# Expert biases as one float32r product of high and low parts, and the residual kept only as its two parts

## The chip, the cores and the metric

The kernel runs on one core of a Trainium2 chip. The metric is device time in microseconds (us), the median of the runs shown; less is better. TensorE (PE) multiplies, VectorE (DVE), ScalarE (ACT) and GpSimd (POOL) work on whole tiles, SyncE (SP) issues most of the DMAs. Each engine takes its instructions in order. "PEld" in the profile is TensorE's loading of weights, which runs beside its products.

## What is computed

One layer of a decoder on 256 tokens of 1024 columns, in float32: token mixing (sparse attention, a sliding window, a gated merge, an output projection, a residual), then 32 experts of which each token uses four, a second residual and a last norm. The change lies in the second half:

```python
def clamped_swiglu(gu):
    x_glu, x_lin = gu[..., ::2], gu[..., 1::2]
    x_glu = jnp.minimum(x_glu, SWIGLU_LIMIT)
    x_lin = jnp.clip(x_lin, -SWIGLU_LIMIT, SWIGLU_LIMIT)
    return x_glu * jax.nn.sigmoid(SWIGLU_ALPHA * x_glu) * (x_lin + 1.0)
...
    def body(y, blk):
        tok, g, e = blk
        xb = ht[tok]
        hid = clamped_swiglu(xb @ w_up[e] + b_up[e])
        out = hid @ w_down[e] + b_down[e]
        return y.at[tok].add(out * g[:, None]), None
...
    x = x + ga1 * (merged @ w_out[l])
    h = rms_norm(x, g_ffn[l]) * (1.0 + sc2) + sh2
    x = x + ga2 * moe_ffn(h, w_router[l], b_router[l], w_up[l], b_up[l], w_down[l], b_down[l])
    return rms_norm(x, g_final)
```

## The kernel before

Attention takes about the first 245 us. Then the router picks the experts, and the 32 experts follow, each with up to 64 tokens. Their weights, 12 chunks of 1 MB per expert (8 up, 4 down), come through 18 slots in SBUF, issued by SyncE as slots come free. The steps of one expert, with the lines of the kernel before:

- Every four experts, `gather` makes one-hot rows of their tokens (`oh`, L838), multiplies them with `xh` and `xl` (L850; the norms at L826), and VectorE and ScalarE turn the result into `XT` (L852, L853). `xh` and `xl` are the high and low parts of the residual x, made in the first part from `xt` (ScalarE's cast at L762, the differences on GpSimd at L764 and L768).
- `up`: for each of the two halves `n` of the hidden units, the bias opens the sum in PSUM (L891: a column of the identity, broadcast, picks one row of `rows` on 64 partitions; gate and linear columns go to two halves of the array, so two products for each n), then four chunks follow (L904), four float32 products each.
- `act`: swiglu for each half (L801, L803, L805 to L807, on VectorE and ScalarE), two transposes (L914) and a copy into `hTe` (L915).
- `down`: four chunks (L924), the first two into the bank "z", the last two into "o". Each bank's sum is cast to float32r by ScalarE (`ohi`, L930), and VectorE makes the difference (`olo`, L931).
- `combine`: scatter products of the high and the low part (L938, L939), four pairs, and VectorE adds each, times the gate, to `y` (L941).

A float32 product counts as two records in the trace, a float32r product as one: a chunk's four up products are x8 there, a down chunk is x16, a bias x8 per expert.

Before expert 16 all engines meet at a branch (L962): a loop over tokens beyond the 64 of an expert, which is not entered here. Its condition is read from `count`.

At the end the second residual comes in: `y` times `g2b` (L1075) plus `xt` (L1076), for both halves of the tokens, then the last expert's down products (L1085) a quarter of the columns at a time, with the last norm behind them, written over `xt` (L1106, L1113, L1115) and out.

The order of the instructions on each engine is not that of the text: a scheduler with a timeline of its own puts them in order when the kernel is built, and an engine then keeps that order, waiting where an operand is late. `issue_after` and one dependency by hand (L891's second half for expert 0, the chunks of expert 16) are the only hints.

Of the kernel before, what the change touches and what calls it, by code (L numbers as in the profile page):

```python
# [10 lines left out]
F32 = mybir.dt.float32  # L11
F32R = mybir.dt.float32r
# [9 lines left out]
SL = 64  # L22
# [58 lines left out]
def _layout(inp):  # L81
# [6 lines left out]
    def pairs(a, b):  # L88
        """blocks of 128 columns by row: [block, column, a | b, row]"""
        return np.stack([a, b], axis=2).reshape(8, 128, 2048)  # L90

    def twos(a):
        """two blocks of 128 columns by row"""
        return a.reshape(4, 2, 128, D).transpose(0, 2, 1, 3).reshape(4, 128, 2048)
# [63 lines left out]
def tile_trunk(ctx: ExitStack, tc: tile.TileContext, A, out: bass.AP, dbg=None):  # L158
# [65 lines left out]
    def residual(i, q, slots):  # L224
        """two blocks of 128 columns of the modulation of a residual"""
# [6 lines left out]
    def across(g, out, tag="pt"):  # L232
        """a vector of columns, on all partitions"""
# [12 lines left out]
    # =====================================================================  # L246
    # token mixing
    # =====================================================================
    with tc.tile_pool(name="front", bufs=1) as fr:
# [5 lines left out]
        def split(src, n, pool=0):  # L255
            """float32 as an exact sum of two float32r parts; the last columns' difference on GpSimd"""
# [14 lines left out]
        # conditioning  # L271
# [8 lines left out]
        # the conditioning vector on all partitions  # L280
# [3 lines left out]
        # rms norm and transposes of x  # L284
# [7 lines left out]
        # relative bias of 16 heads by distance  # L292
# [26 lines left out]
        def modulation(i, k, scale, shift, g):  # L319
            """a block of 128 columns of a scale (times g) and a shift"""  # L320
# [8 lines left out]
        # projections, those with the columns on partitions: kc vc | ksl kw | qn0..3 | qs0..3, and with the tokens  # L329
        # there: vsl vw vs. Each float32 product is three of float32r parts, the product of the low parts being  # L330
        # below float32's last place
# [36 lines left out]
        # as Hankel tiles: the query rows run backwards  # L368
# [20 lines left out]
        def backwards(ap):  # L389
            """the queries of each half in reverse"""  # L390
            return bass.AP(tensor=ap.tensor, offset=ap.offset + 127, ap=[list(z) for z in ap.ap[:-1]] + [[-1, 128]])
# [18 lines left out]
        # branch gates (their eight partial sums in four groups of partitions)  # L410
# [17 lines left out]
        # kc, vc: halves of the partitions take the even and the odd tokens' rows  # L428
# [24 lines left out]
        def transposed(tiles, cols, eng):  # L453
            """the blocks' transposes, side by side: [keys, block, queries]"""
# [14 lines left out]
        def weights(a):  # L469
            """softmax of the selected and window branches, with the branches' gates"""  # L470
# [38 lines left out]
        def compressed(a, po):  # L509
            """closes the sum of the three branches"""  # L510
# [3 lines left out]
            # compressed branch  # L514
# [26 lines left out]
        def sliding(a):  # L541
# [3 lines left out]
            # sliding window with sinks  # L545
# [31 lines left out]
        # ks  # L577
# [9 lines left out]
        # compressed keys and values, hidden layer  # L587
# [19 lines left out]
        # compressed keys and values, second layer  # L607
# [30 lines left out]
        # merge gates, second modulation  # L638
# [21 lines left out]
        # branches' projections, merge  # L660
# [27 lines left out]
        # output projection, residual, router with the second modulation in its weights  # L688
# [81 lines left out]
        # the logits' eight partial sums are in four groups of partitions  # L770
# [27 lines left out]
    def swiglu(pool, gu):  # L798
        """of half of the hidden units"""
# [10 lines left out]
    # =====================================================================  # L810
    # experts
    # =====================================================================
    g2b = fixed([128, D], F32, "g2b", "qn")
    with tc.tile_pool(name="moe", bufs=1) as mo:
# [6 lines left out]
        def norms(oh):  # L821
            """the norms of the slots' tokens, on all partitions"""
# [312 lines left out]
```

## Time and profile before

| | us |
|---|---|
| median of 3 runs | 1216.19 |
| lowest, highest | 1215.51, 1217.31 |
| span of the profiled execution | 1211.7 |
| TensorE busy in it | 1148.3 |
| VectorE, ScalarE, GpSimd busy | 491.8, 234.6, 135.5 |
| weights' DMA (queue of SyncE), share of 16 engines | 93.1% |

The profiled execution's own time is its span; what lies around it is the difference to the median, 4.5 us. Busy time of TensorE includes the modelled ends of pipelined products, so 95% does not say that it never waits: its timeline, start against start, does. Rows of the timeline give the start, the duration, the engine, the line, the operation, the tiles (out<-in), the shapes, the number of instructions merged into the row, and in brackets the idle time before and who ended it.

### The profile page before, as it was taken

How to read it: one execution, taken by the hardware profiler on the slowest of the kernel's cores; microseconds unless marked ns; L12 is line 12 of the kernel's file. 1: busy time of each engine (PE TensorE's matmuls, PEld its weight loads, DVE VectorE, ACT ScalarE, POOL GpSimd, SP SyncE). 2: the span in 40 equal slices, each digit the busy share in tenths (PEclk: the TensorE clock that was granted, in tenths of full speed). 3: DMA queues.
4: the chain of work that ended last, by engine and by line, in shares of the span. 5: the costliest groups of instructions: out<-in, count | busy, mean ns of one | idle time of the engine just before them, and what ended most of it. 6: DMA issues, size and time to landing. Idle time of an engine off the chain costs nothing. (4 is left out here: it accounts for less than half of the span.)

```text
span 1211.7 us, 16366 instructions
## 1 busy us (share of the span) xinstructions
PE 1148.3 (95%) x6645; PEld 587.2 (48%) x6646; DVE 491.8 (41%) x1041; ACT 234.6 (19%) x535; POOL 135.5 (11%) x115
## 2 busy tenths in 40 slices
PE   6999998989999999999999987999999999999996
PEld 5867768934345434434444433445444444443443
DVE  7958687641343332322322232233222323233334
ACT  3346453321102011201111101101111110111002
POOL 4726474400000000000000000000000000000001
PEclk8999998989999999999999998999999999999999
DMA  9988555879999999999999999999999999999993
GB/s 384 412 310 325 209 209 176 314 306 403 388 421 416 422 421 421 421 420 421 421 421 421 421 416 371 420 422 420 422 420 421 422 420 422 421 421 421 420 422 148
DMA packets 66608, 463.79 MB, mean 383 GB/s; under 512 B 7216, under 2 KB 9408, under 8 KB 11744
## 3 DMA queue, kind: packets, MB, share of 16 engines
q1 hardware_dynamic: 66016, 461.84, 93.1%
q8 instruction: 54, 0.88, 0.3%
q10 hardware_dynamic: 512, 0.85, 0.2%
q14 instruction: 26, 0.21, 0.0%
HBM read 461.59 MB, written 1.07 MB: 382 GB/s over the span
## 5 line engine op out<-in xcount | busy, mean ns | idle before, releaser
L904 PE MATMUL z<-chunk,XT 128*64 128x512 f32 x2048 | 476.5, 599 | 0.0
L904 PEld LDWEIGHTS z<-chunk,XT 128*64 128x64 f32 x2048 | 143.9, 137 | 261.9 <-issue 243.0
L941 DVE SCALAR_TENSOR_TENSOR y<-s,gates,y 128x512 f32<-128x512 f32 x124 | 90.9, 748 | 118.9 <-PE s L939 116.3
L924 PE MATMUL z<-chunk,hTe 128*64 128x256 f32 x992 | 124.2, 383 | 8.3 <-ACT hTe L915 8.3
L924 PE MATMUL o<-chunk,hTe 128*64 128x256 f32 x992 | 122.8, 382 | 0.0
L801 DVE TENSOR_SCALAR g<-z 128x256 f32<-128x256 f32 x64 | 27.1, 424 | 234.9 <-PE z L904 234.9
L1106 POOL TENSOR_TENSOR xt<-y,gfb 128x512 f32<-128x512 f32 x3 | 3.9, 1293 | 954.9 <-ACT sq L1105 952.4
L265 POOL TENSOR_TENSOR hilo<-chunk,hilo 128x576 fp32r<-128x576 f32 (+4 forms) x49 | 93.1, 1916 | 78.3 <-ACT hilo L261 55.6
L924 PEld LDWEIGHTS z<-chunk,hTe 128*64 128x64 f32 x992 | 70.6, 136 | 57.9 <-issue 14.6
L803 ACT ACTIVATE th<-g 128x256 f32<-128x256 f32 x64 | 26.7, 416 | 356.8 <-DVE g L801 356.8
L924 PEld LDWEIGHTS o<-chunk,hTe 128*64 128x64 f32 x992 | 71.4, 137 | 39.0 <-issue 6.3
L891 PE MATMUL z<-rows,kc 64*64 64x512 f32 x256 | 67.2, 624 | 6.4 <-PEq L962 6.4
L931 DVE TENSOR_TENSOR olo<-z,ohi 128x512 fp32r<-128x512 f32 x31 | 21.4, 691 | 118.6 <-ACT ohi L930 118.6
L340 PE MATMUL z<-hh,hilo 128*128 128x256 f32 x184 | 53.0, 295 | 8.5 <-ACT hh L350 8.5
L938 PE MATMUL s<-ohi,oht 128*128 128x512 f32 x124 | 56.1, 468 | 4.1 <-DVE y L941 2.7
L261 ACT CAST hilo<-chunk 128x1024 fp32r<-128x1024 f32 (+1 forms) x49 | 49.4, 1029 | 29.9 <-PE z L676 10.0
L341 PE MATMUL z<-hh,hilo 128*128 128x256 f32 x184 | 52.9, 291 | 0.0
L324 DVE SCALAR_TENSOR_TENSOR chunk<-chunk,condrow 128x1024 f32<-128x1024 f32 x32 | 51.3, 1638 | 1.0 <-DMA chunk<-in_wada 1.0
L915 ACT COPY hTe<-pt 128x256 f32<-128x256 f32 x64 | 23.6, 371 | 144.6 <-PE pt L914 144.5
L342 PE MATMUL z<-hl,hilo 128*128 128x256 f32 x184 | 50.8, 290 | 0.8 <-DVE hl L351 0.7
L938 PEld LDWEIGHTS s<-ohi,oht 128*128 128x128 f32 x124 | 22.2, 187 | 57.9 <-issue 35.7
L939 PE MATMUL s<-olo,oht 128*128 128x512 f32 x124 | 48.7, 408 | 0.0
(302 smaller groups left out, 1282.2 us busy)
## 6 DMA issues: line engine op xcount, KB each, us to landing
chunk<-in_wup SPq DMA_DIRECT2D x256, 1024.0 KB, 19.8
chunk<-in_wdn SPq DMA_DIRECT2D x127, 1024.0 KB, 19.8
chunk<-in_wada SPq DMA_DIRECT2D x24, 1024.0 KB, 12.3
chunk<-in_wing SPq DMA_DIRECT2D x8, 1024.0 KB, 6.8
chunk<-in_win SPq DMA_DIRECT2D x7, 960.0 KB, 17.0
chunk<-in_w SPq DMA_DIRECT2D x4, 1024.0 KB, 12.0
chunk<-in_wbr SPq DMA_DIRECT2D x4, 1024.0 KB, 5.3
chunk<-in_wout SPq DMA_DIRECT2D x4, 1024.0 KB, 5.6
```

Of the source, the lines that this page charges most:

```text
L261: ACT.copy(hi[:, 0:n], src)
L265: POOL.tensor_tensor(lo[:, d:n], src[:, d:n], hi[:, d:n].bitcast(F32), op=OP.subtract)
L324: V.scalar_tensor_tensor(w[:, b], w[:, b], 1.0, condrow, op0=OP.mult, op1=OP.mult, accum_out=m[:, b:b + 1])
L340: PE.matmul(o, wh, hh[:, k], start=start, stop=False)
L341: PE.matmul(o, wl, hh[:, k], start=False, stop=False)
L342: PE.matmul(o, wh, hl[:, k], start=False, stop=stop)
L891: PE.matmul(gu[n][64 * c:64 * c + 64], ident[0:64, 2 * e + c:2 * e + c + 1].to_broadcast([64, 64]), rows[0:64, n * 512:(n + 1) * 512], sta ...
L904: PE.matmul(gu[n][64 * c:64 * c + 64], XT[:, 2 * j + k, c0:c0 + 64], w[:, k, c], start=False, stop=j == 3 and k == 1)
L924: PE.matmul(po[j // 2][64 * c:64 * c + 64, (j % 2) * 256:(j % 2) * 256 + 256], hT_[:, b, 64 * c:64 * c + 64], w[:, c, b], start=j % 2 == 0 ...
L938: PE.matmul(p, r[:, a], hi[:, n], start=True, stop=False)
L939: PE.matmul(p, r[:, a], lo[:, n], start=False, stop=True)
L941: V.scalar_tensor_tensor(ys, p, gates[:, a, e:e + 1], ys, op0=OP.mult, op1=OP.add)
```

## The change

The bias of `up` is added behind the chunks by one float32r product over 128 partitions for each half (L903 in the new file): `bias` holds the high parts of the 64 rows on partitions 0 to 63 and the low parts on 64 to 127, and `chosen`, 128x128, picks the two rows of the expert; ScalarE makes it anew for each expert (L888). The first up product now opens the sum. `bias` and `pick` are made once, ahead of the experts, by one copy on ScalarE (L911) and two operations on VectorE (L912, L913), and lie in the slot of `xt`, which is given up: the second residual adds `xh` and `xl` one after the other (L1084), and the last norm writes to a new tile `last` in the slot of `XT`.

```diff
@@ up
             gu = pair("gu")
+            ACT.copy(chosen[e % 2].rearrange("p (c n) -> p c n", c=2),
+                     pick[:, 2 * e:2 * e + 2, None].to_broadcast([128, 2, 64]))
             for n in range(2):
-                with tc.issue_after(fold) if e == 0 and n == 1 else nullcontext():
-                    for c in range(2):
-                        PE.matmul(gu[n][64 * c:64 * c + 64],
-                                  ident[0:64, 2 * e + c:2 * e + c + 1].to_broadcast([64, 64]),
-                                  rows[0:64, n * 512:(n + 1) * 512], start=True, stop=False)
                 for j in range(4):
...
-                            PE.matmul(gu[n][64 * c:64 * c + 64], XT[:, 2 * j + k, c0:c0 + 64], w[:, k, c], start=False,
-                                      stop=j == 3 and k == 1)
+                            PE.matmul(gu[n][64 * c:64 * c + 64], XT[:, 2 * j + k, c0:c0 + 64], w[:, k, c],
+                                      start=j == 0 and k == 0, stop=False)
+                PE.matmul(gu[n], chosen[e % 2], bias[:, n * 512:(n + 1) * 512], start=False, stop=True)
             return gu
+        both = fixed([128, D + 2 * E + 256], F32R, "bias", "xt")
+        bias, pick = both[:, 0:D], both[:, D:D + 2 * E].bitcast(F32)
+        chosen = [both[:, D + 2 * E + 128 * n:D + 2 * E + 128 * n + 128] for n in range(2)]
+        ACT.copy(bias[0:64], rows[0:64])
+        V.tensor_tensor(bias[64:128], rows[0:64], bias[0:64].bitcast(F32), op=OP.subtract)
+        V.tensor_tensor(both[:, D:D + 2 * E], ident[:, 0:64], ident[:, 64:128], op=OP.add)
@@ the second residual and the last norm
             V.tensor_tensor(y[:, a], y[:, a], g2b, op=OP.mult)
-            V.tensor_tensor(y[:, a], y[:, a], xt[:, a], op=OP.add)
+            for part in (xh, xl):
+                V.tensor_tensor(y[:, a], y[:, a], part[:, a].bitcast(F32), op=OP.add)
+        last = fixed([128, 2, D], F32, "last", "XT")
...
-            (V if j == 3 else POOL).tensor_tensor(xt[:, :, cs], y[:, :, cs],
+            (V if j == 3 else POOL).tensor_tensor(last[:, :, cs], y[:, :, cs],
```

The other lines of the diff are comments taken out and `xt` renamed to `last`. In the new file the up products are L901, the transposes of the hidden units L921, the down products L931, the scatter products L945 and L946, the addition to `y` L948; L881 (the one-hot rows of the scattering) keeps its number.

The scheduler puts the instructions into another order, too. TensorE, between the up chunks of expert 30 and the down chunks behind them, before (the names: kc holds the identity, th is swiglu's result, hTe its transpose):

```order
L904 MATMUL z<-chunk,XT 64x512 x3
L924 MATMUL z<-chunk,hTe 64x256 [waits DMAHW1_49,Activation_49]
L924 MATMUL z<-chunk,hTe 64x256 x3
L891 MATMUL z<-rows,kc 64x512 [waits PE_49]
L891 MATMUL z<-rows,kc 64x512
L891 MATMUL z<-rows,kc 64x512 [waits DVE_49,PE_49]
L891 MATMUL z<-rows,kc 64x512
L914 MATMUL pt<-kc,th 128x128 [waits DVE_49]
L914 MATMUL pt<-kc,th 128x128
```

The same place now:

```order
L901 MATMUL z<-chunk,XT 64x512 x3
L903 MATMUL z<-bias 128x512
L931 MATMUL z<-chunk,hTe 64x256 [waits DMAHW1_49,Activation_49]
L931 MATMUL z<-chunk,hTe 64x256 x3
L921 MATMUL pt<-kc,th 128x128 [waits DVE_49]
L921 MATMUL pt<-kc,th 128x128
```

The next expert's bias stood between the down products and the transposes; now nothing stands there, and a bias product stands ahead of the down products.

TensorE a little later, from the second half of expert 30's down chunks to the first up chunk of expert 31, before:

```order
L924 MATMUL o<-chunk,hTe 64x256 [waits DMAHW3_49]
L924 MATMUL o<-chunk,hTe 64x256 x7
L938 MATMUL s<-ohi,oht 128x512 [waits DVE_49,Activation_49]
L939 MATMUL s<-olo,oht 128x512 [waits DVE_49]
L924 MATMUL o<-chunk,hTe 64x256 [waits DMAHW4_49]
L924 MATMUL o<-chunk,hTe 64x256 x7
L904 MATMUL z<-chunk,XT 64x512 [waits DMAHW5_49]
L904 MATMUL z<-chunk,XT 64x512 x3
L938 MATMUL s<-ohi,oht 128x512 [waits Activation_49]
L938 MATMUL s<-ohi,oht 128x512 [waits DVE_49]
```

The same place now:

```order
L945 MATMUL s<-ohi,oht 128x512 [waits DVE_49,Activation_49]
L931 MATMUL o<-chunk,hTe 64x256 [waits DMAHW3_49]
L931 MATMUL o<-chunk,hTe 64x256 x7
L946 MATMUL s<-olo,oht 128x512 [waits DVE_49]
L931 MATMUL o<-chunk,hTe 64x256 [waits DMAHW4_49]
L931 MATMUL o<-chunk,hTe 64x256 x7
L945 MATMUL s<-ohi,oht 128x512 [waits Activation_49]
L945 MATMUL s<-ohi,oht 128x512 [waits DVE_49]
L946 MATMUL s<-olo,oht 128x512
L901 MATMUL z<-chunk,XT 64x512 [waits DMAHW5_49]
```

The first scatter product moved ahead of the third down chunk, and three more moved ahead of the next expert's first up chunk; each waits for ScalarE's cast of the sum that ended just before it.

VectorE at the end, from expert 30's last additions to the swiglu of expert 31, before:

```order
L941 SCALAR_TENSOR_TENSOR y<-s,gates,y 128x512 [waits PE_49] x2
L1075 TENSOR_TENSOR y<-y,g2b 128x1024 [waits DVE_49]
L941 SCALAR_TENSOR_TENSOR y<-s,gates,y 128x512 [waits PE_49]
L1076 TENSOR_TENSOR y<-y,xt 128x1024 [waits DVE_49]
L1075 TENSOR_TENSOR y<-y,g2b 128x1024 [waits DVE_49]
L1076 TENSOR_TENSOR y<-y,xt 128x1024 [waits DVE_49]
```

The same place now:

```order
L948 SCALAR_TENSOR_TENSOR y<-s,gates,y 128x512 [waits PE_49] x3
L1082 TENSOR_TENSOR y<-y,g2b 128x1024 [waits DVE_49] x2
L1084 TENSOR_TENSOR y<-y,xh 128x1024 [waits DVE_49] x2
L1084 TENSOR_TENSOR y<-y,xl 128x1024 [waits DVE_49] x2
```

Two operations are new, and the first multiplication moved behind the last addition.

## Rows read from the trace of the kernel before

**Rows 1.** The page's chain of waits, shares of the span by engine.
```profile
PE 35%; DVE 3%; ACT 1%; issue 0%; POOLq 0%; DVEq 0%; ACTq 0%
```
**Rows 2.** Stretches: busy time by engine, TensorE's granted clock, DMA share, GB/s.
```profile
250.00:731.00 481.00, 463.69 (x2557) 203.09 (x2556) 151.10 (x306) 63.73 (x144) 0.00 (x0) 0.99 0.99 410
712.00:727.90 15.90, 11.83 (x82) 6.09 (x76) 6.39 (x11) 1.96 (x4) 0.00 (x0) 1.00 1.02 424
...
731.00:735.00 4.00, 1.53 (x4) 0.58 (x6) 0.76 (x2) 0.00 (x0) 0.00 (x0) 0.50 0.34 102
735.00:1190.00 455.00, 445.45 (x2464) 195.18 (x2462) 139.53 (x271) 56.59 (x128) 0.00 (x0) 0.99 1.01 420
```
**Rows 3.** SyncE's issues of expert 31's up chunks; the weights' time to landing.
```profile
1145.52 17.80 SPq L193 DMA_DIRECT2D chunk<-in_wup  x8
...
DMA to landing us min/median/max: 17.4/19.8/19.8
```
**Rows 4.** Timeline of TensorE, experts 30 and 31.
```profile
1151.67 5.37 PE L904 MATMUL z<-chunk,XT 128*64 128x512 f32 x24
...
1162.82 1.03 PE L924 MATMUL z<-chunk,hTe 128*64 128x256 f32 x8
1163.78 1.93 PE L891 MATMUL z<-rows,kc 64*64 64x512 f32 x8
1165.64 0.44 PE L914 MATMUL pt<-kc,th 128*128 128x128 f32 x2
...
1166.54 2.81 PE L924 MATMUL z<-chunk,hTe 128*64 128x256 f32 x24 [0.24 <-ACT hTe L915]
...
1173.45 1.89 PE L904 MATMUL z<-chunk,XT 128*64 128x512 f32 x8
1175.27 0.73 PE L938 MATMUL s<-ohi,oht 128*128 128x512 f32 x2
...
1178.92 1.51 PE L904 MATMUL z<-chunk,XT 128*64 128x512 f32 x6
```
**Rows 5.** Timeline of TensorE, expert 15, the last ahead of the branch.
```profile
712.70 1.03 PE L924 MATMUL z<-chunk,hTe 128*64 128x256 f32 x8
714.71 0.44 PE L914 MATMUL pt<-kc,th 128*128 128x128 f32 x2 [0.98 <-DVE th L807]
...
715.61 2.81 PE L924 MATMUL z<-chunk,hTe 128*64 128x256 f32 x24 [0.24 <-ACT hTe L915]
719.16 0.50 PE L938 MATMUL s<-ohi,oht 128*128 128x512 f32 x1 [0.74 <-ACT ohi L930]
719.60 1.95 PE L924 MATMUL o<-chunk,hTe 128*64 128x256 f32 x16
...
724.53 0.73 PE L938 MATMUL s<-ohi,oht 128*128 128x512 f32 x2 [0.69 <-ACT ohi L930]
725.10 0.65 PE L939 MATMUL s<-olo,oht 128*128 128x512 f32 x2
```
**Rows 6.** Timeline of TensorE between experts 1 and 2.
```profile
302.56 1.07 PE L891 MATMUL z<-rows,kc 64*64 64x512 f32 x4
303.57 1.07 PE L904 MATMUL z<-chunk,XT 128*64 128x512 f32 x2
```
**Rows 7.** Timeline of GpSimd, the last reading of x ahead of the experts.
```profile
243.80 1.27 POOL L768 TENSOR_TENSOR xl<-xt,xh 128x512 fp32r<-128x512 f32 x1 [5.87 <-ACT xh L762]
```
**Rows 8.** Timeline behind the branch, VectorE and TensorE.
```profile
733.15 0.76 DVE L838 TENSOR_TENSOR oh<-kc,posm 128x256 fp32r<-128x256 f32 x2 [5.29 <-PEq L962]
...
733.47 3.68 PE L891 MATMUL z<-rows,kc 64*64 64x512 f32 x8 [6.40 <-PEq L962]
```
**Rows 9.** Timeline of VectorE and TensorE, the second residual and expert 31's swiglu.
```profile
1179.70 1.22 DVE L1076 TENSOR_TENSOR y<-y,xt 128x1024 f32<-128x1024 f32 x1
...
1183.23 0.42 DVE L801 TENSOR_SCALAR g<-z 128x256 f32<-128x256 f32 x1
...
1185.12 0.41 PE L914 MATMUL pt<-kc,th 128*128 128x128 f32 x2 [0.82 <-DVE th L807]
```

More of the change, by code (lines that the diff above doesn't have):

```diff
@@ L1112, in tile_trunk @@
             cs = slice(n * 512, n * 512 + 512)
-            V.tensor_scalar(xt[:, 0, cs], xt[:, 0, cs], r3[:, 0:1], None, op0=OP.mult)
-            nc.sync.dma_start(out[0:128, cs], xt[:, 0, cs])
-            ACT.mul(xt[:, 1, cs], xt[:, 1, cs], r3[:, 1:2])
-            nc.scalar.dma_start(out[128:256, cs], xt[:, 1, cs])
+            V.tensor_scalar(last[:, 0, cs], last[:, 0, cs], r3[:, 0:1], None, op0=OP.mult)
+            nc.sync.dma_start(out[0:128, cs], last[:, 0, cs])
+            ACT.mul(last[:, 1, cs], last[:, 1, cs], r3[:, 1:2])
+            nc.scalar.dma_start(out[128:256, cs], last[:, 1, cs])
 def kernel(**inputs):
```

## The prediction

> **What bounds the kernel now.** I read the chain of waits first: the piece that ended last runs from the branch in the middle to the end and is almost all TensorE [rows 1]. The stretches then show the DMA at 420 GB/s on both sides of that branch, with one hole around it: 102 GB/s for 4.0 us, about 3 us of transfer lost [rows 2]. So two things run side by side at their limit, and the question is which one waits. Expert 31's first weight chunk is issued at 1145.52 and a chunk takes 19.8 us to land, so it lies there from 1165.3 [rows 3]; TensorE takes it at 1173.45 [rows 4]. TensorE is some 8 us behind the data, even at the end of the expert stage, where the gap is smallest. **The bound is TensorE's own stream, in order, with its waits inside it**; the DMA is a floor a little below. Whatever the change does to that stream, per expert, shows in the time; what it does to the DMA only shows if the 8 us are used up.
>
> One expert's stream in the late experts, from the third up chunk of expert 30 (1151.67) to that of expert 31 (1178.92), is 27.25 us [rows 4].
>
> **The bias products.** Removed: four float32 products per expert (eight records). In the late order they stand between the first half of a down chunk and the transposes of the second half of the hidden units, 1163.78 to 1165.64, 1.86 us [rows 4]. They sit where TensorE would wait anyway: those transposes need VectorE's swiglu. Expert 15, which has no bias products behind it because of the branch, shows that place without them: from the down products at 712.70 to the transposes at 714.71 is 2.01 us [rows 5], against 1162.82 to 1165.64, 2.82 us, with them [rows 4]. Taking them away gives 0.8 us, not 1.86. With the bias product right in front, swiglu begins when it ends, about 0.2 us sooner relative to the down products than in rows 5; so the gain here is 1.0.
>
> Added: two float32r products of 512 columns per expert. The nearest rows are the scatter products: one alone between float32 work takes 0.44 us of the stream (719.16 to 719.60) [rows 5], and the float32 work before it ends about 0.15 later than in a run of its own kind (1.82 for a chunk before a scatter product, 1173.45 to 1175.27, against 5.37/3 or less in a run) [rows 4]. I take 0.6 each, 1.2 per expert, bounds 0.44 and 0.65. The first of them also delays swiglu of the first half, and TensorE waits about 0.15 more for its transposes.
> By the Trainium skill's "FP8 and Floating Point Precision" (TensorE Precision Notes) true FP32 takes four passes through the array; by that alone one pass for four would leave a quarter of 1.86, about 0.5 us per expert, and the change would give back 1.4 us each time. Rows 4 and 5 speak against it, as most of the 1.86 covers a wait.
>
> **The order behind it.** The change also moves the scatter products (now L945, L946). Before, the order after the last down product of a half is more down products or an up chunk, and the scatter product comes behind that, when ScalarE has cast the result. Now it stands directly behind, in most experts from 9 on: once after the first half of the down chunks, once before the next expert's first up chunk. Expert 15 has this very order in the kernel before, and its rows price it: TensorE sits idle 0.74 and 0.69 us for ScalarE's cast, at 719.16 and 724.53 [rows 5]. From the second down products (715.61) to the pair at 725.10 is 9.49, and two more scatter products and a switch (0.33) bring the next up chunk to 9.8; in expert 30 that way is 1166.54 to 1173.45, 6.9 [rows 4]. Part comes back behind it: from the first up chunk to the third takes 5.47 now (1173.45 to 1178.92) with five scatter products in between [rows 4]; with three, 1.82 + 0.90 + 1.75 = 4.5. Together +1.9 us.
> The Trainium skill's "PSUM — Partial Sum Buffer" (Engine vs sequencer instructions) says that matmuls start and complete in program order; the two idle times in rows 5, with ready chunks behind them, agree. So a waiting scatter product holds everything behind it.
>
> A late expert then is: order +1.9, two new products and the 0.15 they add less the switches already counted +0.95, old bias gone −1.0: **27.25 becomes about 29.1, +1.85.** The group of four around a gathering varies: where the gathering's products fill the first new wait, +0.7; the next one, whose second transposes were covered by gathering anyway and which gets no new cast wait at the end, −1.4; the one behind it +2.2; the fourth +1.8. That is +3.3 per four. Experts 7 to 15 come to +7.0 (7 and 8 +1.2, 9 +1.3, 10 +0.3, 11 −0.9, 12 +1.7, 13 +1.9, 14 +1.8, 15 −0.3), experts 24 to 30 to +9.1. Late experts: **+16.1**.
>
> **The experts in the other order.** In experts 1 to 6 and 17 to 23 (the first in each half) up chunks cover the waits, so the bias is plain work: 1.0 us for one half (302.56 to 303.57) [rows 6], 2.0 per expert, against 1.2 now. Six of them gain the whole 0.8, −4.8. The other seven lose part of it to a wait (the second transposes, the copy of the hidden units): −2.9. Together **−7.7**.
>
> **The start.** Expert 0's bias ran while TensorE waited for the router; now 1.2 us of it are in the stream, and since both halves' swiglu then come close together, 0.4 more: +1.6. VectorE gets the subtraction of the low parts (L912, 64x1024) in the router's chain, in front of the search for indices. It waits for ScalarE's high parts (L911), which wait until GpSimd has read x for the last time, at 243.80 + 1.27 [rows 7]; ScalarE's copy of 1024 columns is done about when VectorE gets there. Queued behind it are the indices, the one-hot rows and the gathering of expert 0, and TensorE waits for these. An addition of 1024 columns takes 1.13 to 1.23 us (from the spacing at the end, below), so +1.2. Less work in this gap may keep TensorE at half clock longer, as at the branch: +0.5, bounds 0 and 1.7. **+3.3**.
>
> **The middle.** Behind the branch eight bias records took 3.68 us at half clock, before the gathering [rows 8]; they go, but the one-hot rows of the gathering are begun at 733.15 and not ready before about 734.7 [rows 8], and its own products then run at half clock longer: −0.8 (bounds −2.4 and 0); expert 16's new products +1.2. **+0.4**. The DMA hole grows or shrinks with TensorE's arrival, but TensorE does not wait for it.
>
> **The end.** VectorE now does six operations of 1024 columns where it did four, all behind the last accumulation. The last accumulation is followed by 1179.70, and swiglu begins at 1183.23 after three of them, 1.18 each [rows 9]. TensorE waits for it: the transposes come at 1185.12, 0.82 idle [rows 9]. Now six of them, begun about 2.6 us earlier in the stream because the last scatter products come a chunk earlier: +1.25 at the down products, −0.2 at the second transposes. **+1.05**. If the cover of that one chunk were gone, +3.4.
> ScalarE's copy of the chosen columns (128x128, every expert) stands between two steps of swiglu while VectorE is at the step before: 0. Bounds 0 and 0.3 each.
>
> Sum: +16.1 − 7.7 + 3.3 + 0.4 + 1.05 = **+13.15 us**. The profiled execution has a span of 1211.7, 4.5 below the median of 1216.19; I add the sum to the median: **1229.3 us**.
>
> **The rivals.**
> 1. The saving goes through (faster). If TensorE's waits are shorter than in rows 5, say because ScalarE's casts are earlier, the bias work gives 0.7 us in each of 30 experts, 20 us. Then the DMA floor decides, from the point where the 8 us of distance are gone: its hole of 3 to 4 us closes, and about 9 us go in all: 1207. By the four passes of the Trainium skill's page on FP8 and floating point, named above, the gain would be larger, with the same floor. Against it: the order of rows 5 is exactly the new one. Chance 0.12.
> 2. No change. The early gains and late losses are of opposite sign; if the late order costs 0.9 per expert instead of 1.85 (one wait covered instead of none), 16.1 becomes about 4 and the sum is 1 us: 1217. Chance 0.06.
> 3. The waits pull the clock down. TensorE's granted clock fell to half around the branch, where products took twice as long (3.68 for 1.86) [rows 4, 8]. With some 3 us of waits per expert the late stage could fall too: two stretches like that per group of four, 1.7 each, in five groups, +17: 1246. The Trainium skill's "TensorE: Matmul & The Clock Gate" (Part 1) says the throttled state is the default and activity lifts it. Against it: expert 15's stretch, 4 of 15.9 us idle, has clock 1.00 [rows 2]. Chance 0.04.
>
> **How the numbers follow.** Forecast 0.78, rivals 0.12, 0.06, 0.04. The forecast's own range, from the bounds above (late experts ±0.5 each over 14, ±7; start and middle ±2; end 0 to +3), is 1219 to 1238, and the tails outside hold the rest. The range 1218 to 1238 leaves out rival 1, rival 3, part of rival 2. A measurement tells 0.2%, 2.4 us, from no change: faster 0.12, same 0.06, slower 0.82.
>
> **What would show it.** In the changed kernel: a plain late expert's period near 29.1; a wait for ScalarE's cast at L945, twice per expert, some 0.7 each; the second transposes (L921) waiting about 0.9 for VectorE where bias products stood; the middle branch reached some 9 us later; DMA still at 420 outside the hole. Wrong would be: periods of 27 or less, or TensorE waiting for chunks.

## The result

The changed kernel takes **1223.66 us** (median of four runs, 1222.98 to 1224.68); the kernel before, run beside it, 1215.85 (four runs, 1213.47 to 1217.31). The ratio is **1.0072, 95% interval 1.0057 to 1.0087**: slower by some 8 us. The forecast was 1229.3, range 1218 to 1238, slower at 0.82.

The profiled executions have spans of 1222.7 and 1211.7 us, 11.0 apart. Runs of one kernel spread over 2 to 5 us, and the profiled run of before was one of its short ones; so the whole is taken from the runs, and the places from the two traces.

This table gives where expert 0, 1, 7, ... starts (its first up chunk on TensorE, us from the span's start) in the profiled run of every kernel of this document, and the span. The experiments e1 to e8 are explained below.

```
                    e0     e1     e7    e15    e17    e24     e31    span
before           254.2  277.2  463.6  696.1  761.6  975.1  1173.5  1211.7
after            257.0  279.7  462.7  704.4  766.1  972.9  1181.4  1222.7
e1 order kept    256.7  279.4  461.1  691.2  760.8  968.3  1167.2  1210.0
e2 before, new   255.4  280.0  466.4  713.3  777.7  991.2  1201.2  1237.9
e3 residual only 253.9  277.0  463.3  695.8  761.2  974.8  1173.0  1215.1
e4 entry later   254.0  276.6  462.0  703.8  764.5  975.0  1183.6  1223.1
e5 order, end    255.7  278.4  460.1  690.1  760.0  967.6  1166.7  1210.1
e6 all three     254.1  276.8  462.0  690.8  760.6  971.4  1168.3  1210.6
e7 before, b16   254.6  277.7  464.0  696.5  762.6  978.1  1176.4  1214.7
e8 no products   256.5  280.1  454.6  682.3  761.3  965.1  1167.8  1211.2
```

From its first two lines, stretch by stretch, beside the terms of the prediction:

```
stretch                             predicted   measured
start and expert 0                     +3.3       +2.5
experts 1 to 6                     }              -3.4
experts 17 to 23                   }   -7.7       -6.7
experts 7 to 14                        +7.3       +9.2
expert 15, the branch, expert 16       +0.1       -3.8
experts 24 to 30                       +9.1      +10.1
expert 31 and the end                  +1.05      +3.1
sum                                   +13.15     +11.0
```

**The profile after.** The chain of waits, shares of the span by engine [rows 1]: TensorE still carries it, and the waits of ScalarE and DMA in it stay small.

```profile
PE 33%; DVE 3%; ACT 1%; DMA 1%; issue 1%; SPq 0%; POOLq 0%; DVEq 0%; ACTq 0%
```

Groups by line (operation, shape and count; busy time and mean ns; idle time of the engine just before, and who ended most of it), the scatter products of the high part first in the kernel before, then in the changed one: over the whole kernel TensorE's idle time in front of them grows from 4.1 to 24.4 us, 17.0 of it waiting for ScalarE's cast. In front of the transposes of the hidden units it waits 17.2 us for VectorE.

```profile
L938 PE MATMUL s<-ohi,oht 128*128 128x512 f32 x124 | 56.1, 468 | 4.1 <-DVE y L941 2.7
L945 PE MATMUL s<-ohi,oht 128*128 128x512 f32 x124 | 53.6, 455 | 24.4 <-ACT ohi L937 17.0
L921 PE MATMUL pt<-kc,th 128*128 128x128 f32 x128 | 26.9, 292 | 18.5 <-DVE th L807 17.2
```

The timeline of TensorE, experts 29 and 30, the place of [rows 4]:

```profile
1123.03 1.94 PE L901 MATMUL z<-chunk,XT 128*64 128x512 f32 x8
...
1131.09 0.50 PE L903 MATMUL z<-bias 128*128 128x512 f32 x1
1131.52 1.94 PE L901 MATMUL z<-chunk,XT 128*64 128x512 f32 x8
...
1139.60 1.08 PE L931 MATMUL z<-chunk,hTe 128*64 128x256 f32 x8
1141.50 0.44 PE L921 MATMUL pt<-kc,th 128*128 128x128 f32 x2 [0.82 <-DVE th L807]
...
1145.95 0.49 PE L945 MATMUL s<-ohi,oht 128*128 128x512 f32 x1 [0.74 <-ACT ohi L937]
...
1151.32 0.72 PE L945 MATMUL s<-ohi,oht 128*128 128x512 f32 x2 [0.69 <-ACT ohi L937]
...
1152.21 1.08 PE L901 MATMUL z<-chunk,XT 128*64 128x512 f32 x4
```

From first up chunk to first up chunk, 1123.03 to 1152.21, is 29.18 us, where it was 27.25 [rows 4]. The three waits, 0.82, 0.74 and 0.69, stand where the prediction put them, and the last two have the sizes of [rows 5]. A new bias product takes 0.43 of the stream (1131.09 to 1131.52).

The stretches (busy time of five engines, TensorE's granted clock, DMA share, GB/s), beside [rows 2]: ahead of the branch the DMA is no longer full, since SyncE issues a chunk when TensorE has freed its slot, and TensorE is late; behind it, it is full again; and a half clock stands near the end.

```profile
690.00:720.00 30.00, 27.44 (x150) 11.08 (x148) 7.99 (x15) 3.05 (x7) 0.00 (x0) 1.00 0.85 346
...
745.00:1150.00 405.00, 385.17 (x2139) 171.02 (x2139) 121.95 (x244) 55.74 (x132) 0.00 (x0) 1.00 1.01 421
...
1195.00:1199.00 4.00, 4.00 (x14) 1.19 (x12) 0.00 (x0) 0.00 (x0) 0.00 (x0) 0.57 0.37 150
```

The end, VectorE and then TensorE, beside [rows 9]: six operations of 1024 columns (three rows of two) before swiglu of the last expert, and TensorE 2.00 us idle for it, then at half clock (the 24 records of up products take 7.07 us, where 24 took 5.37 at full clock [rows 4]).

```profile
1185.14 2.35 DVE L1082 TENSOR_TENSOR y<-y,g2b 128x1024 f32<-128x1024 f32 x2
1187.41 2.35 DVE L1084 TENSOR_TENSOR y<-y,xh 128x1024 f32<-128x1024 f32 x2
1189.68 2.35 DVE L1084 TENSOR_TENSOR y<-y,xl 128x1024 f32<-128x1024 f32 x2
1191.95 0.41 DVE L801 TENSOR_SCALAR g<-z 128x256 f32<-128x256 f32 x1
```
```profile
1193.83 0.41 PE L921 MATMUL pt<-kc,th 128*128 128x128 f32 x2 [2.00 <-DVE th L807]
1194.17 7.07 PE L901 MATMUL z<-chunk,XT 128*64 128x512 f32 x24
```

### The profile page after: what moved, and what is told of

Its sections match the earlier page's. It is cut to its first block, busy times and chain, and to the rows that moved or that the text cites. A ratio compares the mean times of both kernels' runs of the same rounds, so it can differ in the third digit from the quotient of the medians.

```text
span 1222.7 us, 16026 instructions
## 1 busy us (share of the span) xinstructions
PE 1123.4 (92%) x6453; PEld 580.1 (47%) x6454; DVE 495.1 (40%) x1045; ACT 244.6 (20%) x568; POOL 135.7 (11%) x115
## 5 line engine op out<-in xcount | busy, mean ns | idle before, releaser
L901 PE MATMUL z<-chunk,XT 128*64 128x512 f32 x2048 | 478.4, 600 | 0.7 <-DMA chunk<-in_wup 0.5
L901 PEld LDWEIGHTS z<-chunk,XT 128*64 128x64 f32 x2048 | 140.5, 137 | 254.8 <-issue 244.3
L948 DVE SCALAR_TENSOR_TENSOR y<-s,gates,y 128x512 f32<-128x512 f32 x124 | 90.5, 747 | 119.8 <-PE s L946 119.6
L931 PE MATMUL z<-chunk,hTe 128*64 128x256 f32 x992 | 123.3, 385 | 10.0 <-ACT hTe L922 10.0
L931 PE MATMUL o<-chunk,hTe 128*64 128x256 f32 x992 | 121.0, 382 | 0.0
L1115 POOL TENSOR_TENSOR last<-y,gfb 128x512 f32<-128x512 f32 x3 | 3.9, 1316 | 965.0 <-ACT sq L1114 962.8
L931 PEld LDWEIGHTS z<-chunk,hTe 128*64 128x64 f32 x992 | 67.4, 136 | 54.0 <-ACT hTe L922 16.7
L931 PEld LDWEIGHTS o<-chunk,hTe 128*64 128x64 f32 x992 | 69.7, 137 | 38.5 <-issue 7.4
L945 PE MATMUL s<-ohi,oht 128*128 128x512 f32 x124 | 53.6, 455 | 24.4 <-ACT ohi L937 17.0
L946 PE MATMUL s<-olo,oht 128*128 128x512 f32 x124 | 51.6, 424 | 0.0
L945 PEld LDWEIGHTS s<-ohi,oht 128*128 128x128 f32 x124 | 21.9, 187 | 60.6 <-ACT ohi L937 28.4
L921 PE MATMUL pt<-kc,th 128*128 128x128 f32 x128 | 26.9, 292 | 18.5 <-DVE th L807 17.2
L937 ACT CAST ohi<-z 128x512 fp32r<-128x512 f32 x31 | 18.2, 586 | 128.1 <-PE z L931 105.0
```

Of the source, the lines that this page charges most:

```text
L901: PE.matmul(gu[n][64 * c:64 * c + 64], XT[:, 2 * j + k, c0:c0 + 64], w[:, k, c], start=j == 0 and k == 0, stop=False)
L921: PE.transpose(p[:, b], t[:, b * 128:(b + 1) * 128], ident)
L931: PE.matmul(po[j // 2][64 * c:64 * c + 64, (j % 2) * 256:(j % 2) * 256 + 256], hT_[:, b, 64 * c:64 * c + 64], w[:, c, b], start=j % 2 == 0 ...
L945: PE.matmul(p, r[:, a], hi[:, n], start=True, stop=False)
L946: PE.matmul(p, r[:, a], lo[:, n], start=False, stop=True)
L948: V.scalar_tensor_tensor(ys, p, gates[:, a, e:e + 1], ys, op0=OP.mult, op1=OP.add)
```

## The experiments

**e1: the changed products in the old order.** A note on each issue of a scatter product says which product it must follow (marked `behind`), so that the order is that of before in the late experts.

```
     combine(e, r, hi, lo), for a, for n:
-        PE.matmul(p, r[:, a], hi[:, n], start=True, stop=False)
-        PE.matmul(p, r[:, a], lo[:, n], start=False, stop=True)
+        with tc.issue_after(behind[max(a, n)]) if e % MID != MID - 1 else nullcontext():
+            PE.matmul(p, r[:, a], hi[:, n], start=True, stop=False)
+            PE.matmul(p, r[:, a], lo[:, n], start=False, stop=True)
     behind[0]: the last product of this expert's third down chunk
     behind[1]: the last product of the next expert's first up chunk
```

> The changed kernel, with its scatter products (L945, L946) held back to the places that they had before: the first pair of an expert behind its third down chunk, the others behind the next expert's first up chunk. The new bias products stay. If the order is the cause: a plain late expert falls from 29.2 to about 27.3 us, and the kernel from 1223.7 to about 1207, or to 1207 to 1211 where the DMA floor holds it. If the new products or the lost cover of the old ones are the cause: the period stays near 29 and the time within 2 us of 1223.7.

Measured: **1210.34 us** (before beside it 1213.82), ratio 0.9969, interval 0.9957 to 0.9980. TensorE's timeline, experts 29 and 30:

```profile
1135.53 0.50 PE L950 MATMUL s<-ohi,oht 128*128 128x512 f32 x1
1135.87 0.40 PE L951 MATMUL s<-olo,oht 128*128 128x512 f32 x1
1136.19 1.95 PE L933 MATMUL o<-chunk,hTe 128*64 128x256 f32 x16
1137.97 1.89 PE L901 MATMUL z<-chunk,XT 128*64 128x512 f32 x8
1139.79 0.73 PE L950 MATMUL s<-ohi,oht 128*128 128x512 f32 x2
...
1152.17 1.08 PE L901 MATMUL z<-chunk,XT 128*64 128x512 f32 x4 [0.44 <-DMA chunk<-in_wup]
```

Neither wait for the cast is left, and the expert from 1110.7 to 1137.97 takes 27.3 us. Everything else of the change is still there. So the order alone makes the 1.9 us per late expert. By expert 30 TensorE has caught up with the chunks (the last row). That the transfers then set the end is what e5, e6 and e8 test.

**e2: the old products in the new order.** The kernel before, its eight bias records kept; in ten experts one high product is put between the second and third down chunk, and in these and two more, three products ahead of the next up chunk.

```
 down(e, hT_, r):
+    early = e in (8, 9, 10, 12, 13, 14, 24, 25, 26, 28, 29, 30)
     for j in range(4):
+        with tc.issue_after(h0) if h0 and j == 2 else nullcontext():
             ... the products of chunk j
+        if j == 1 and early and e not in (10, 26):
+            h0 = PE.matmul(p0, r[:, 0], hi[:, 0], start=True, stop=False).ins
...
+    ... r[:, 0] with hi[:, 1], r[:, 1] with hi[:, 0] and lo[:, 0]; the next expert's first up chunk behind them
```

> The kernel before, with its old bias products, but in experts 8 to 10, 12 to 14, 24 to 26 and 28 to 30 the scatter products stand where the changed kernel has them: one between the second and third down chunk, three ahead of the next expert's first up chunk. If the order is the cause: a plain late expert goes from 27.25 to about 29.1 us and the kernel from 1215.9 to 1231 to 1236. If it is not: 27.25 and 1216.

Measured: **1237.37 us** against 1213.82, ratio 1.0186, interval 1.0168 to 1.0203. TensorE's timeline, experts 29 and 30:

```profile
1142.85 1.94 PE L905 MATMUL z<-chunk,XT 128*64 128x512 f32 x8
...
1165.74 0.50 PE L949 MATMUL s<-ohi,oht 128*128 128x512 f32 x1 [0.74 <-ACT ohi L945]
...
1171.11 0.50 PE L955 MATMUL s<-ohi,oht 128*128 128x512 f32 x1 [0.69 <-ACT ohi L945]
...
1172.01 1.51 PE L905 MATMUL z<-chunk,XT 128*64 128x512 f32 x6
```

The same two waits, and 1142.85 to 1172.01 is 29.16 us in place of 27.25: the kernel before with nothing changed but the order loses the same 1.9. With e1 this settles the main term from both sides. The whole is 1.4 us above the expected band, and the band was counted from 1215.9: the +23.6 measured here is 3.5 above the most that it allowed. In experts 8 and 9 the enforced order made the scheduler move other products too (3.6 and 4.9 us there), and expert 1 starts 2.8 later, as the clock behind the router is at half for longer in 253 to 256 us (granted clock 0.62, 1.00 in before) and again from 275.7 to 279.1 (0.51).

**e3: the residual part alone.** In the kernel before, two lines and a destination.

```
-            V.tensor_tensor(y[:, a], y[:, a], xt[:, a], op=OP.add)
+            for part in (xh, xl):
+                V.tensor_tensor(y[:, a], y[:, a], part[:, a].bitcast(F32), op=OP.add)
+        last = fixed([128, 2, D], F32, "last", "XT")
```

> The kernel before with the residual part alone: the end adds the high and the low parts (six VectorE operations of 1024 columns for four), the last product goes to its own place. No product is moved. The prediction's price without a cover: swiglu of the last expert 2.4 us later, the end +2.4, so 1218 (1217 to 1219.5). Rival, that the additions are hidden behind the last expert's up chunks: 1216 and no wait over 0.9 us at the last transposes.

Measured: **1218.44 us** against 1213.82, ratio 1.0032, interval 1.0020 to 1.0043. All of it is behind expert 31's first up chunk, which starts 0.5 sooner than in before (1173.0 for 1173.5). The timeline of VectorE and TensorE, the last of the six additions and the transposes; then the stretch behind:

```profile
1184.50 1.21 DVE L1077 TENSOR_TENSOR y<-y,xl 128x1024 f32<-128x1024 f32 x1
...
1186.73 0.41 PE L914 MATMUL pt<-kc,th 128*128 128x128 f32 x2 [2.84 <-DVE th L807]
1187.07 7.07 PE L904 MATMUL z<-chunk,XT 128*64 128x512 f32 x24
```
```profile
1187.00:1191.00 4.00, 4.00 (x14) 1.21 (x14) 0.00 (x0) 0.37 (x1) 0.00 (x0) 0.57 0.68 278
```

TensorE waits 2.84 us where it waited 0.82 [rows 9]: +2.0, near the two additions of 1.18 each. Then the granted clock falls to half (0.57 over the stretch), and the 24 records of up products take 7.07 us, where 24 took 5.37 [rows 4]: another 1.7. That is 3.7 of the 3.8 us that the two traces differ by behind expert 31's start. So the price without a cover (+3.4 in the prediction, +2.4 in the expectation) counted additions alone, and of these 2.0 came; that the sum is near 3.4, and the time in the expected band, is luck: the half clock was in neither, and the band was counted from 1215.9 where before stands at 1213.8 here. No run has the bias part alone: its tables lie where x lay.

**e4: the entry.** The two preparing steps of VectorE are issued behind the one-hot rows.

```
-        V.tensor_tensor(bias[64:128], rows[0:64], bias[0:64].bitcast(F32), op=OP.subtract)
-        V.tensor_tensor(both[:, D:D + 2 * E], ident[:, 0:64], ident[:, 64:128], op=OP.add)
...
         with tc.issue_after(first[1]):
+            V.tensor_tensor(bias[64:128], rows[0:64], bias[0:64].bitcast(F32), op=OP.subtract)
+            V.tensor_tensor(both[:, D:D + 2 * E], ident[:, 0:64], ident[:, 64:128], op=OP.add)
             weigh()
```

> The changed kernel with VectorE's two preparing steps (low parts of the biases, L912, and the columns to choose from, L913) issued behind the one-hot rows of the first gathering in place of ahead of the indices. If these steps delay the entry: expert 0's first up chunk starts 1.2 us sooner (257.0 to 255.8), or 2.8 sooner if the half clock behind the router is shorter too; the whole 1 to 3 us less, 1221 to 1222.5. If the entry's loss is the clock alone: 257.0. The order of the scatter products also shifts in experts 18 to 23 with this edit, so the entry is read in the trace, and the whole may differ by another 2 us.

Measured: expert 0 starts at 254.0, 3.0 sooner than in the changed kernel. The stretch 253 to 256, first of the changed kernel, then of e4:

```profile
253.00:256.00 3.00, 3.00 (x14) 2.82 (x14) 1.89 (x8) 1.30 (x3) 0.00 (x0) 0.50 0.01 3
```
```profile
253.00:256.00 3.00, 3.00 (x18) 1.48 (x18) 2.25 (x9) 2.33 (x5) 0.00 (x0) 1.00 0.01 3
```

So the steps do delay the entry, and the half clock makes 3.0 us of 1.2. But the whole got no better, where 1 to 3 us less was expected: **1227.26 us**, ratio 1.0110, interval 1.0093 to 1.0126. Half of the 3 us is gone by expert 2, where e4 has a stretch at half clock of its own (0.50 from 300.0 to 303.4), and 0.6 is left at expert 15; from expert 17 to 24, where the edit also moved scatter and down products, e4 takes 210.5 us, the changed kernel 206.8. The miss of the whole is thus mostly another order of work, not the entry.

e4 shows one thing more, at its end. The same wait of 2.00 us stands in front of the same transposes as in the changed kernel, but the clock stays at 1.00 and the 24 records behind it take 5.37 us:

```profile
1195.98 0.41 PE L919 MATMUL pt<-kc,th 128*128 128x128 f32 x2 [2.00 <-DVE th L807]
1196.32 5.37 PE L901 MATMUL z<-chunk,XT 128*64 128x512 f32 x24
```

**e5 and e6: what is left at the end, and at the entry.** e5 is e1 with the additions of the low parts behind the last expert's one-hot rows, a quarter of the columns at a time; e6 has the edit of e4 too.

```
-            for part in (xh, xl):
-                V.tensor_tensor(y[:, a], y[:, a], part[:, a].bitcast(F32), op=OP.add)
+            V.tensor_tensor(y[:, a], y[:, a], xh[:, a].bitcast(F32), op=OP.add)
...
+            with tc.issue_after(behind[2]):
+                V.tensor_tensor(y[:, :, cs], y[:, :, cs], xl[:, :, cs].bitcast(F32), op=OP.add)
```

> The changed kernel with the scatter products held back as in e1, and the low parts of x added at the end behind the last expert's swiglu and its one-hot rows (four VectorE operations of 512 columns) in place of ahead of it. If the two more additions ahead of swiglu cost the end: the last expert's second transposes wait 0.9 us in place of 2.0, no half clock follows, and the whole is 2 to 3 us below e1's 1210.3, at 1207 to 1208.5. If the end is paced by its chunks alone: 1210, as e1.

> e5 with the two preparing steps of VectorE moved behind the one-hot rows as in e4. Expert 0 starts at 254.0 in place of 256.7. If chunks are issued earlier by that and the late stage is paced by their landing: 2 to 3 us below e5, 1204.5 to 1206.5. If the transfers before expert 0 set the pace of what follows, whenever expert 0 starts: as e5, 1207 to 1208.5.

Measured: **1212.32** and **1212.33 us** against 1214.41; ratios 0.9980 (0.9970 to 0.9990) and 0.9977 (0.9967 to 0.9987). Neither is better than e1's 0.9969 (0.9957 to 0.9980). In e5's last expert the local aim is reached, with no long wait at the transposes and a granted clock of 1.00 from 1150 to 1190; but TensorE waits for chunks instead. TensorE's timeline of e5, and the stretch:

```profile
1179.11 1.94 PE L901 MATMUL z<-chunk,XT 128*64 128x512 f32 x8
1181.59 1.94 PE L901 MATMUL z<-chunk,XT 128*64 128x512 f32 x8 [0.55 <-DMA chunk<-in_wup]
1184.07 1.94 PE L901 MATMUL z<-chunk,XT 128*64 128x512 f32 x8 [0.54 <-DMA chunk<-in_wup]
```
```profile
1150.00:1190.00 40.00, 35.29 (x187) 13.57 (x185) 15.29 (x26) 3.54 (x8) 0.00 (x0) 1.00 1.00 414
```

Up chunks follow each other at 2.48 us, the transfer's pace, for 1.94 us of products. The second reading of each expectation, that the transfers set the end, is the one that came, though the times given with it, 1210 and 1207 to 1208.5, were 2 to 4 us too low. In e6 the head start of the entry is spent at the branch, where the first up chunk comes after a wait of 4.09 us (4.39 in e5); experts 17 to 23 then take 3.2 us more than in e5, and that does not move the end either.

**e7: the bias of expert 16 behind its up products, in the kernel before.** This tests the middle: are the eight records behind the branch [rows 8] on the path?

```
+                    if e != MID:
+                        biases(n)          # as before, ahead of the up products
...
+                if e == MID:
+                    biases(n)              # behind them
```

> The kernel before, but expert 16's eight bias records stand behind its up products and not ahead of the gathering behind the branch. If the whole of these 3.6 us was on the path there: expert 16's first up chunk 3.5 to 4 us sooner (743.6 to about 739.8), of which 1.9 go back for the same records at full clock later: the whole -2 us, ratio 0.998 to 0.999. If the one-hot rows cover them, as the prediction had it: at most 2.4 sooner, and no gain in all, ratio 1.000.

Measured: **1216.55 us** against 1214.41, ratio 1.0018, interval 1.0008 to 1.0028: slightly slower. TensorE's timeline:

```profile
740.69 1.94 PE L908 MATMUL z<-chunk,XT 128*64 128x512 f32 x8
743.79 1.94 PE L908 MATMUL z<-chunk,XT 128*64 128x512 f32 x8 [1.16 <-DMA chunk<-in_wup]
746.28 1.94 PE L908 MATMUL z<-chunk,XT 128*64 128x512 f32 x8 [0.55 <-DMA chunk<-in_wup]
748.75 1.94 PE L908 MATMUL z<-chunk,XT 128*64 128x512 f32 x8 [0.53 <-DMA chunk<-in_wup]
```

The first up chunk is taken at 740.7 in place of 743.6. That is 2.9 us sooner, between the two readings; the gathering's first product comes after 6.71 us of idle time, the records came after 6.40 [rows 8], and expert 15 started 0.4 later than in before, which together make up nearly the 3.68. So the records were on the path there and no one-hot row covered them. But the next chunks have not landed: 2.2 us of waits, and the 2.0 us of bias records are now plain work. In the kernel before, the bias records covered a wait for chunks. Neither reading of the expectation had this.

**e8: no bias products at all.** e5 without the product of L903. The up projections' biases are missing from what it computes.

```
-                PE.matmul(gu[n], chosen[e % 2], bias[:, n * 512:(n + 1) * 512], start=False, stop=True)
```

> The kernel of e5 with the two new bias products of every expert left out (the up projections' biases are then missing from the result). It prices the products, and whether anything but the transfers sets the end. Price: a plain late expert, 27.3 us in e5, comes to 26.1 to 26.3, by 0.43 of each product and 0.1 to 0.15 of its switches. The end: if the landing of the last chunks sets it, the whole stays at e5's 1212.3 (1210 to 1213, ratio 0.996 to 0.999) though some 30 us of TensorE's work are gone; if TensorE's stream still sets it: 1195 to 1203.

Measured: **1212.38 us** against 1215.03, ratio 0.9977, interval 0.9967 to 0.9986, the same as e5. TensorE's timeline around expert 12, and of expert 30; then the chain of waits by engine:

```profile
598.78 1.94 PE L901 MATMUL z<-chunk,XT 128*64 128x512 f32 x8
...
625.28 1.03 PE L901 MATMUL z<-chunk,XT 128*64 128x512 f32 x4
...
1152.85 1.94 PE L901 MATMUL z<-chunk,XT 128*64 128x512 f32 x8 [0.55 <-DMA chunk<-in_wup]
...
1157.92 1.08 PE L932 MATMUL z<-chunk,hTe 128*64 128x256 f32 x8 [0.64 <-DMA chunk<-in_wdn]
```
```profile
PE 22%; DMA 13%; DVE 3%; ACT 1%; issue 1%; SPq 0%; POOLq 0%; DVEq 0%; ACTq 0%
```

Where TensorE is the bound, an expert is 26.50 us (598.78 to 625.28) for 27.3 in e5: two new bias products with their switches cost **0.8 us** (1.0 to 1.2 was expected). Expert 15 starts 7.8 us sooner than in e5, and expert 17 1.3 us later; the end is the same to 0.1 us. In its late experts the period is 30.0 us (1106.6 to 1136.6), which is twelve chunks at 2.49. Some 25 us less work on TensorE leave the end where it was: the transfers set it in both.

## Right and wrong, step by step

**The bound: right for the changed kernel.** TensorE's own stream with its waits set the time of the changed kernel: in its trace the up products wait for a chunk once, 0.55 us (behind the branch). Matmuls start in program order, says the Trainium skill's "PSUM — Partial Sum Buffer" (Engine vs sequencer instructions); e1 and e2 agree, since the place of four short products moved each late expert by 1.9 us, both ways.

**The late experts: right.** Predicted 29.1 us, measured 29.18; the order +1.9 as predicted (e1, e2), the new products 0.8 for a net 0.95 (e8), the lost cover as predicted: from the first half down chunk to the transposes is now 1.90 (1139.60 to 1141.50) for 2.82 [rows 4], 0.9 of the 1.86 saved. (So about half of the 1.86 covered a wait, not most of it; and a new product takes 0.4 with its switches, not 0.6: the 0.15 that I added for a change of kind is 0.03 in the rows given for it, 1.82 against 5.37/3.) The wait appeared in place of the work that had filled it. The groups came to +9.2 and +10.1 for 7.3 and 9.1; of the missing 2.9, experts 7 and 8 alone are 1.6 (+2.8 for +1.2).

**Experts 1 to 6 and 17 to 23: sign right, too small.** −10.1 for −7.7. I had kept back 2.7 of 13 times 0.8 for waits that would take the place of the work. In sum nearly all of the 10.4 came, but not evenly: 3.4 of 4.8 in the six, 6.7 for 5.6 in the seven, so the 0.8 is not the price of every expert. e8 comes nearest to it: without the two new products experts 1 to 6 take 7.2 us less than in e5, of which up to 1.7 is a stretch at half clock that only e5 has there (0.51 from 360.7 to 364.1). That leaves 0.9 to 1.2 each, where 1.2 was predicted. What the other experts gained beyond 0.8 no run takes apart.

**The start: right in sum, by two errors.** Expert 0 begins 2.8 late, not 1.7: the half clock took the upper end of its bound, 1.7 for 0.5 (e4 shows both parts go with VectorE's steps). Expert 0 itself lost nothing where I had +1.6: its stretch in before also held half of expert 1's bias, 1.0 us (276.23 to 277.24), which went. That the two errors cancel is luck.

**The middle: wrong.** I took the one-hot rows for a cover of 2.9 of the 3.7 us of bias records. There was none: in the changed kernel the norms' products begin after 6.31 us of idle time, the bias records had begun after 6.40 [rows 8]. I had misread the row: its 0.76 us are both one-hot operations together, so they end at 733.9, not at 734.7, and the first of them is enough to begin.

```profile
741.55 1.19 PE L826 MATMUL s<-oh,r 128*128 128x256 f32 x2 [6.31 <-DVE oh L838]
```

All of it went, −3.8 for +0.1. And it could go because TensorE was 8 us late and the chunks had landed. e1 and e7 reach the same place sooner and give the gain back in waits for chunks; in e1 the first up chunk:

```profile
740.47 7.07 PE L901 MATMUL z<-chunk,XT 128*64 128x512 f32 x24 [3.75 <-DMA chunk<-in_wup]
```

In e1, e5, e6 and e8 expert 16 starts with such a wait, between 739.7 and 740.9, whenever expert 15 started (682.3 to 691.2). The prediction says that TensorE does not wait for the DMA there, and looked for the data's lead at the end of the kernel only, 8 us; at the branch of the kernel before it was 4.8 (a chunk issued at 733.85 landed 4.9 us later, and TensorE took it at 743.59).

**The end: mechanism right, too small.** The wait grew to 2.00 us from 0.82, +1.2 as predicted. Missed were 1.7 us of half clock behind it, the third rival's mechanism, once and at another place than I named. It isn't a sure price of that wait: e4 has the wait and not the half clock.

**The sum and the base.** The sum is 2.15 us too high, beside the 11.0 between the spans. That is in part luck: the late experts and the end came 4.95 higher than forecast, the early experts, the middle and the start 7.1 lower. The forecast is 5.6 too high. 1.9 of it is the sum, beside the 11.2 us between the two profiled runs (1213.47 and 1224.68). 2.7 is that I added the sum to the median of three runs, 1216.19, while the span it was worked out from belonged to the short run of 1213.47. The last 1.0 is that the changed kernel's profiled run was the longest of its four. The kernel before came to 1213.8, 1214.4 and 1215.0 in later sets of 13 to 25 runs. That 0.2% I should have had in the range only.

**The rivals.** The first (the saving goes through) needed the order of before; e1 has it, and reaches the floor as the rival said. But the floor is 1210 to 1212, not 1207: 2 to 3.5 us below before in the same sets, not 9. Two of its steps fail. TensorE, once it has caught up, takes expert 31 at the transfers' pace: from its first up chunk to the end e5 needs 43.4 us, before 38.2. And the hole in the transfers does not close: from 720 to 745 us the DMA moved 359 GB/s in before and 337 in e1.

```profile
720.00:745.00 25.00, 17.33 (x91) 10.36 (x89) 8.69 (x17) 4.64 (x10) 0.00 (x0) 0.80 0.88 359
```
```profile
720.00:745.00 25.00, 13.37 (x56) 9.01 (x58) 8.06 (x16) 4.69 (x10) 0.00 (x0) 0.80 0.83 337
```

What holds it open can be read in the traces. SyncE stands at the branch in waits of its own, here in before and in e1 (us in total, times, longest):

```profile
SPq L962 <- SPq L962: 9.1, 5, 2.5
```
```profile
SPq L976 <- SPq L976: 15.0, 7, 3.1
```

They end one chunk at a time, as the chunks that it issued ahead of the branch land. Its next issue comes when the last of them has landed, however long TensorE has been there (us; "TensorE" is where its last product ahead of the branch starts):

```
          TensorE   last issue ahead   to landing   landed   next issue
before      726.7         723.89           9.9       733.8     733.85
after       734.8         732.06           7.8       739.9     739.97
e1          722.7         719.87          15.5       735.4     735.50
e8          715.8         715.98          19.9       735.9     735.95
```

The next chunk lands 4.8 to 5.0 us behind that issue in all four, where a full queue gives one in 2.5. So the queue runs empty once at the branch, in every kernel, and reaching it sooner can't help while the transfers ahead of it are still on their way. Expert 31's last chunk is issued no sooner in e1 (1177.10) than in before (1175.35).

The second rival needed a late order that costs 0.9 us per expert; it cost 1.9. The third needed a half clock in the late stage; from 745 to 1150 us it was 1.00.

The fastest kernel here is e1, 0.9969 of before; the intervals of e5, e6 and e8 overlap with its. The change's arithmetic is worth having once the order is kept; what it saves beyond some 3 us the transfers don't let through.

## What to carry to other kernels

Before counting saved products, look at what stands behind them: work that fills a wait is worth only what it exceeds the wait by (0.9 of 1.86 us here), and a scheduler that sees other work may place the next products where they wait (1.9 us per expert, twice those 0.9). When an edit changes costs, compare the issue order first, and pin the order that was good. And look for the distance to the floor at its narrowest place in the whole kernel, not only at the end: a branch at which the issuing engine waits for its transfers to land is such a place.

## What the runs showed of the hardware beyond that

TensorE's clock can fall to half behind a single idle stretch inside busy work. It did behind 2.00 us (the changed kernel, 1195 to 1199, mean granted clock 0.57) and 2.84 us (e3, 1187 to 1191, 0.57), and the wait that was 1.2 us longer than before cost 2.9 in the changed kernel. It did not behind the same 2.00 us in e4 (1196 to 1200, 1.00). Behind the waits of 0.7 to 0.8 us, three in every plain late expert of the changed kernel, it stayed at 1.00. Nor is one long wait needed: in the kernel before it stood at half from 436.9 to 440.3 (0.50), and the longest wait in the 12 us ahead was 0.61. What decides, no run takes apart.

Two products of 128x512 in float32r with their switches cost 0.8 us of stream (e8), for 1.86 us of the eight float32 records that they replace.
